# A bidirectional RWKV-7 step: the triangular inversion on two partitions a block, and values and keys turned by VectorE and SBUF transfers in place of PE transposes

## The chip, the cores and the metric

The kernel runs on one core of a Trainium2 chip, in float32. The metric is the device time of one execution in microseconds. PE is the matmul engine, DVE the vector engine, ACT the scalar engine, POOL GpSimd, and SP the engine that issues nearly all DMA transfers. Each engine works through its own instructions in the order in which they stand in its program.

## The reference

One layer: h = modulated RMSNorm(x) for 384 tokens (128 of context, 256 latent), z = h @ w_in, then an RWKV-7 scan in both directions over 32 heads of 64, a short convolution, gates and output projections.

```python
def step(S, inp):
    r_t, w_t, k_t, v_t, a_t, b_t = inp
    sa = jnp.einsum('dbhij,dbhj->dbhi', S, a_t)
    S = S * w_t[..., None, :] + sa[..., :, None] * b_t[..., None, :] + v_t[..., :, None] * k_t[..., None, :]
    y = jnp.einsum('dbhij,dbhj->dbhi', S, r_t)
    return S, y
...
y_a = (y.astype(h.dtype) * jax.nn.silu(g_a)) @ w_out_a
y_b = (b_gate * u * jax.nn.silu(g_b)) @ w_out_b
merged = jax.nn.sigmoid(m_a) * y_a + jax.nn.sigmoid(m_b) * y_b
return merged @ w_o, S_fin
```

The scan is computed by chunks of 64 tokens (6 chunks, two directions, two heads: 24 triangular systems of 64 x 64 in a block of two heads). Each needs the inverse of a unit triangular matrix, which is built from 32 x 32 blocks.

## The kernel before

**The stream.** All large projections run through one stream of matmuls on PE (class Stream). It works on pairs of 128 columns: rk (receptance and keys of a block), gv (gate of the block and values of the next), ma, mb, bc, bx, bg, gb and so on, h against 2048 rows of weights. A step is three matmuls on a 128 x 128 tile (mm3: hi*hi, hi*lo, lo*hi; lines 81 to 83), a pair has 32 steps. The weights of half a pair are loaded into a tile raw (two buffers, wload, L101 or, in two pieces, L104), and split quarter by quarter into whi (ACT, L88) and wlo (DVE, L89), three buffers each: wlo_gv_0_0 is the first quarter of gv, wlo_gv_1_0 the third. A step needs both parts of its quarter.

**The blocks.** The scan is done for 16 blocks of two heads, b = 0 to 15. For each the main loop runs generators that put their own matmuls between the steps of the stream; a yield of n lets n steps go. prep_b makes the masked products A (pA on PE, A on DVE), stores their 32 x 32 diagonal blocks to DRAM (ui), loads them as U with one diagonal block on each of 48 partitions, inverts all 48 with 30 pairs of DVE instructions (a product into ut, a sum into U), stores the result (uo) and loads it back into A; x11 takes its transposes. prep_c turns the values (6 transposes on PE to pv, copied by ACT to sav) and the scaled keys (10 transposes to pb, copied to bt). prep_a of the next block follows when gv is done (pl, pn), and the stream is let go until the window of 80 steps between prep_b and the scan is full. Then scan runs: pav, pH, pX and the chains of po, pq and pu.

**What sets the order.** PE's order is written out by hand (manual_schedule). DVE, ACT, POOL and SP are ordered when the program is built: the builder's scheduler takes, at each moment of its own reckoning, the earliest written instruction that it holds ready, and issue_after keeps one behind another. That order is fixed in the program; the chip does not change it. In the loop 160 steps make a block: rk and gv are the first two whole pairs after the second pA, then three of the other pairs.

Results of rk are taken by take_shifted: ACT copies the product to zs and scales it to r or k (L417, L418), DVE adds the neighbours with four instructions each (L422, L424). v comes from gv's second half in the same way.

## Time and profile before

| | us |
|---|---|
| median of 3 runs (2234.74 to 2237.2) | 2236.57 |
| the profiled execution, its own time | 2234.36 |
| its span, first to last instruction | 2232.6 |
| DVE inversion, products (480) and sums (480), busy | 154.8 and 154.5 |
| ACT copies of pv and pb, busy | 30.3 and 25.1 |
| PE transposes to pb, and to pv (values, reversed values), busy | 27.9, 7.8 and 7.9 |
| landing of U (192 KB), uo (192 KB) and A (48 KB), median | 5.1, 4.7 and 3.6 |
| mean granted clock of PE | 0.998 |

Times of an engine's groups are unions of their instructions and overlap with other groups of the same engine. In the rows of a timeline the first number is the start in us from the beginning of the span, the second the length; a bracket at the end gives idle time of the engine before the row and what ended it. SPq rows are the issue of transfers, not their flight. Line numbers are those of the kernel before.

### The profile page before, as it was taken

What the parts mean: (1) busy time and instruction counts of PE and PEld (TensorE: products, weight loads), DVE (VectorE), ACT (ScalarE), POOL (GpSimd) and SP (SyncE); (2) the same over time, 40 slices, a digit from 0 to 9 for tenths busy, and PEclk for the clock granted to TensorE, in tenths of its full rate; (3) what the DMA queues carried; (4) which work ended last, traced back from release to release, by engine and by line L of the source; (5) the groups of instructions that cost most, each with busy time, mean ns of one, the idle gap of its engine ahead of it and who ended that gap; (6) DMA issues with size and microseconds to landing.
All of it is one profiled execution on the core that took longest, in us unless ns stands there. A gap on an engine that the chain in (4) does not pass through costs nothing.

```text
span 2232.6 us, 40518 instructions
## 1 busy us (share of the span) xinstructions
PE 2173.1 (97%) x16020; PEld 2062.7 (92%) x16020; DVE 1553.3 (70%) x3240; ACT 1013.5 (45%) x1784; POOL 115.7 (5%) x113
## 2 busy tenths in 40 slices
PE   5999999999999999999999999999999999999998
PEld 3589999999999999999999999999999999998988
DVE  3259567787878878777878787887777785444354
ACT  4245435454545454444445454546454633333333
POOL 2000000000000000000000000000000000000000
PEclk9999999999999999999999999999999999999999
DMA  9974454444343435343444434344445464886633
GB/s 338 346 211 128 131 141 116 116 117 118 108 132 107 130 100 131 106 130 100 121 108 127 112 107 133 107 122 126 124 118 139 144 196 143 294 281 233 220 132 113
DMA packets 426574, 335.25 MB, mean 150 GB/s; under 512 B 82496, under 2 KB 408720, under 8 KB 425488
## 3 DMA queue, kind: packets, MB, share of 16 engines
q1 hardware_dynamic: 424896, 330.91, 50.2%
q8 instruction: 126, 2.06, 0.4%
q10 hardware_dynamic: 432, 1.57, 0.2%
q14 instruction: 64, 0.52, 0.1%
q0 software_dynamic: 1056, 0.19, 0.1%
HBM read 305.80 MB, written 26.21 MB: 149 GB/s over the span
## 4 chain that ended last, share of the span: by engine, by line
PE 74%; DVE 12%; DMA 6%; ACT 4%; issue 2%; SPq 1%; POOL 0%; POOLq 0%; DVEq 0%; ACTq 0%
DMA raw_adah<-in_ada_w_dram 4%; PE d_rk L81 3%; PE d_rk L82 3%; PE d_rk L83 3%; PE d_gv L81 3%; PE d_gv L82 3%; PE d_gv L83 3%; PE d_oa L81 2%; PE pA L703 2%; PE d_oa L83 2%; PE d_oa L82 2%; PE d_mb L81 2%; PE d_mb L83 2%; PE d_mb L82 2%; PE d_bc L81 2%
## 5 line engine op out<-in xcount | busy, mean ns | idle before, releaser
L724 DVE TENSOR_TENSOR ut<-U 48x30 f32<-48x30 f32 (+14 forms) x480 | 154.8, 323 | 18.3 <-DMA U<-ui 5.5
L81 PE MATMUL d_rk<-h_hi,whi_rk 128*128 128x384 f32 x480 | 161.7, 337 | 0.6 <-ACT lst L554 0.6
L726 DVE TENSOR_TENSOR U<-U,ut 48x30 f32<-48x30 f32 (+14 forms) x480 | 154.5, 322 | 11.1
L81 PE MATMUL d_gv<-h_hi,whi_gv 128*128 128x384 f32 x480 | 160.6, 335 | 0.0
L82 PE MATMUL d_rk<-h_lo,whi_rk 128*128 128x384 f32 x480 | 160.5, 334 | 0.0
L83 PE MATMUL d_rk<-h_hi,wlo_rk 128*128 128x384 f32 x480 | 160.4, 334 | 0.0
L83 PE MATMUL d_gv<-h_hi,wlo_gv 128*128 128x384 f32 x480 | 160.4, 334 | 0.0
L82 PE MATMUL d_gv<-h_lo,whi_gv 128*128 128x384 f32 x480 | 160.4, 334 | 0.0
L88 ACT CAST whi_gv<-raw_gv 128x1024 fp32r<-128x1024 f32 (+1 forms) x64 | 64.0, 999 | 139.6 <-PE d_rk L82 100.0
L88 ACT CAST whi_rk<-raw_rk 128x1024 fp32r<-128x1024 f32 x60 | 63.0, 1054 | 110.8 <-PE d_rk L82 34.7
L89 DVE TENSOR_TENSOR wlo_rk<-raw_rk,whi_rk 128x1024 fp32r<-128x1024 f32 x60 | 72.9, 1218 | 45.3 <-ACT whi_rk L88 35.6
L81 PE MATMUL d_bc<-h_hi,whi_bc 128*128 128x384 f32 x256 | 92.2, 360 | 0.0
L81 PE MATMUL d_gb<-h_hi,whi_gb 128*128 128x384 f32 x256 | 92.2, 360 | 0.0
L81 PE MATMUL d_bg<-h_hi,whi_bg 128*128 128x384 f32 x256 | 92.2, 360 | 0.0
L81 PE MATMUL d_bx<-h_hi,whi_bx 128*128 128x384 f32 x256 | 92.1, 360 | 0.0
L81 PE MATMUL d_ma<-h_hi,whi_ma 128*128 128x384 f32 x256 | 91.6, 358 | 0.0
L81 PEld LDWEIGHTS d_rk<-h_hi,whi_rk 128*128 128x128 f32 x480 | 90.1, 188 | 0.9 <-ACT lst L554 0.9
L81 PE MATMUL d_mb<-h_hi,whi_mb 128*128 128x384 f32 x256 | 90.4, 353 | 0.0
L81 PEld LDWEIGHTS d_gv<-h_hi,whi_gv 128*128 128x128 f32 x480 | 90.1, 188 | 0.2
L81 PE MATMUL d_ob<-ybh,whi_ob 128*128 128x384 f32 x256 | 88.4, 345 | 2.0 <-DVE smb L521 1.0
L82 PEld LDWEIGHTS d_rk<-h_lo,whi_rk 128*128 128x128 f32 x480 | 90.2, 188 | 0.0
L82 PEld LDWEIGHTS d_gv<-h_lo,whi_gv 128*128 128x128 f32 x480 | 90.1, 188 | 0.0
(315 smaller groups left out, 6548.4 us busy)
## 6 DMA issues: line engine op xcount, KB each, us to landing
raw_adah<-in_ada_w_dram SPq DMA_DIRECT2D x64, 512.0 KB, 8.7
raw_rk<-in_w_in_dram SPq DMA_DIRECT2D x60, 512.0 KB, 5.3
raw_gv<-in_w_in_dram SPq DMA_DIRECT2D x60, 512.0 KB, 4.9
raw_ma<-in_w_in_dram SPq DMA_DIRECT2D x16, 1024.0 KB, 5.6
raw_mb<-in_w_in_dram SPq DMA_DIRECT2D x16, 1024.0 KB, 5.6
raw_bc<-in_w_in_dram SPq DMA_DIRECT2D x16, 1024.0 KB, 5.5
raw_bx<-in_w_in_dram SPq DMA_DIRECT2D x16, 1024.0 KB, 5.4
raw_bg<-in_w_in_dram SPq DMA_DIRECT2D x16, 1024.0 KB, 5.5
```

Source lines behind the costliest of these rows:

```text
L81: TE.matmul(out, wh, xh, start=start, stop=False)
L82: TE.matmul(out, wh, xl, start=False, stop=False)
L83: TE.matmul(out, wl, xh, start=False, stop=stop)
L88: S.copy(hi[0:rows], src)
L89: V.tensor_tensor(lo[0:rows], src, hi[0:rows].bitcast(F32), ALU.subtract)
L703: TE.matmul(pas[h, n // 4 * 4][:, n % 4, :], bk[hss[h], n, :], pr[hss[h], n, :], start=True, stop=True)
L724: V.tensor_tensor(tv, U[:, 0:s, s:s + 1].broadcast_to([48, s, w]), U[:, s:s + 1, s + 1:].broadcast_to([48, s, w]), ALU.mult)
L726: V.tensor_tensor(U[:, 0:s, s + 1:], U[:, 0:s, s + 1:], tv, ALU.add)
```

## The change

The inversion uses two partitions for a 32 x 32 block. un holds all rows of the block on partitions 0 to 47 and again on 64 to 111; ux holds the even rows of it on the first and the odd rows on the second set, so each of the 30 column steps works on half the rows in one instruction over 112 partitions. There are two loads of un, two of ux and two stores of uo, where there were one and one. The values and the scaled keys are turned in 32 x 32 blocks by DVE (vt, and bks in place), and 8 transfers for sav and 16 for bt, issued by SP, put the blocks in place within SBUF. The transposes to pv and pb and their ACT copies are gone. prep_c gives 24, 16 and 1 steps to the stream in place of its seven; the window stays 80.

```diff
+        box["raw"] = x.ins
...
+    un = sp.tile([112, 32, 32], F32, tag="un", name="un")
+    ux = sp.tile([112, 16, 32], F32, tag="ux", name="ux")
...
+        vt = sp.tile([P, 2, T], F32, tag="vt", name=f"vt_{b}")
+        with tc.issue_after(last):
+            for d in range(2):
+                V.transpose(vt[:, d], v_[b][:, ::-1] if d else v_[b][:])
+            for d in range(2):
+                V.transpose(flat(bks[:, d]), flat(bks[:, d]))
...
-        nc.sync.dma_start(U[:], ui[:].rearrange("d e i s t -> (d e i) s t"))
+        for g in range(2):
+            nc.sync.dma_start(un[64 * g:64 * g + 48], ui[:].rearrange("d e i s t -> (d e i) s t"))
+        for g in range(2):
+            o["loaded"] = nc.sync.dma_start(ux[64 * g:64 * g + 48], ui[:].rearrange(
+                "d e i (m g) t -> (d e i) m g t", g=2)[:, :, g, :]).ins
+        ut = sp.tile([112, 128], F32, tag="ut", name=f"ut_{b}")
         for s in range(1, 31):
-            w = 31 - s
...
+            w, m = 31 - s, (s + 1) // 2
+            tv = ut[:, 0:m * w].rearrange("p (a b) -> p a b", b=w)
+            V.tensor_tensor(tv, ux[:, 0:m, s:s + 1].broadcast_to([112, m, w]),
+                            un[:, s:s + 1, s + 1:].broadcast_to([112, m, w]), ALU.mult)
+            V.tensor_tensor(ux[:, 0:m, s + 1:], ux[:, 0:m, s + 1:], tv, ALU.add)
+        for g in range(2):
+            dg = ux[64 * g:64 * g + 48].rearrange("p a b -> p (a b)")[:, g:512:34]
+            V.tensor_scalar(dg, dg, 1.0, None, ALU.add)
+            nc.sync.dma_start(uo[:].rearrange("d e i (m g) t -> (d e i) m g t", g=2)[:, :, g, :],
+                              ux[64 * g:64 * g + 48])
+        x11 = un[0:64, 0:24, :]
...
-                TE.transpose(pv[:, q, :], src[:, q * P:(q + 1) * P], ident)
...
-                    TE.transpose(pb[:, n - n0, :], o["bk"][d][:, n, :], ident)
-                S.copy(bt[:, NCH * d + n0:NCH * d + n1, :], pb[:, 0:n1 - n0, :])
...
+        with tc.issue_after(o["loaded"]):
+            for e in range(2):
+                for q in range(4):
+                    nc.sync.dma_start(sav[C + 32 * e:C + 32 * e + 32, :, 32 * q:32 * q + 32],
+                                      x[32 * q:32 * q + 32, :, e, :])
+        x = o["bks"][:].rearrange("p d n t -> p (d n) t")
+        for p in range(4):
+            if p % 2 == 0:
+                yield (24, 16)[p // 2]
+            with tc.issue_after(box["raw"]):
+                for q in range(4):
+                    nc.sync.dma_start(bt[32 * p:32 * p + 32, :, 32 * q:32 * q + 32],
+                                      x[32 * q:32 * q + 32, :, 32 * p:32 * p + 32])
```

PE's order loses the transposes and keeps the rest, with the first block's pl and pn some steps later. The order of the other engines moves in more places, shown here for the eleventh block (b = 10), where bg follows gv.

On DVE, around the end of the pair rk: r_ and k_ are the shifts of rk's results, ut with U (or ux) the inversion, wlo_gv_0_0 and wlo_gv_0_1 the splits of the first two quarters of gv. wlo_gv_0_0 stands nine rows ahead of the first of these. Before:

```order
L89 TENSOR_TENSOR wlo_gv_0_1_13421<-raw_gv_0_13413,whi_gv_0_1_13420 128x1024
L726 TENSOR_TENSOR U_13198<-U_13198,ut_13200 48x14x17
L724 TENSOR_TENSOR ut_13200<-U_13198 48x240
L726 TENSOR_TENSOR U_13198<-U_13198,ut_13200 48x15x16
L422 SCALAR_TENSOR_TENSOR r_13460<-zs_13461,par,r_13460 128x127
L724 TENSOR_TENSOR ut_13200<-U_13198 48x240
L424 SCALAR_TENSOR_TENSOR r_13460<-zs_13461,par,r_13460 128x127
```

And now, from the second shift of k on:

```order
L425 SCALAR_TENSOR_TENSOR k_13455<-zs_13456,par,k_13455 128x127
L746 TENSOR_TENSOR ux<-ux,ut_13200 112x9x13
L423 SCALAR_TENSOR_TENSOR k_13455<-zs_13456,par,k_13455 128x255
L744 TENSOR_TENSOR ut_13200<-ux,un 112x120
L425 SCALAR_TENSOR_TENSOR k_13455<-zs_13456,par,k_13455 128x255
L746 TENSOR_TENSOR ux<-ux,ut_13200 112x10x12
L606 TENSOR_TENSOR lo_bs_13496<-kd_0_12705,bsh_13495 128x384
L744 TENSOR_TENSOR ut_13200<-ux,un 112x110
L89 TENSOR_TENSOR wlo_gv_0_0_13384<-raw_gv_0_13380,whi_gv_0_0_13383 128x1024
L746 TENSOR_TENSOR ux<-ux,ut_13200 112x10x11
L89 TENSOR_TENSOR wlo_gv_0_1_13388<-raw_gv_0_13380,whi_gv_0_1_13387 128x1024
```

Both splits have moved from ahead of the shifts to behind the last of them; 20 rows of the inversion follow, and behind those stand both splits of gv's second half.

On ACT, from the end of rk to the start of bg: zs, r, k and v are the copies and scalings of rk's and gv's results, whi the casts. Before:

```order
L88 CAST whi_gv_0_0_13416<-raw_gv_0_13413 128x1024
L88 CAST whi_gv_0_1_13420<-raw_gv_0_13413 128x1024
L417 COPY zs_13461<-d_rk_0_13342 128x384
L418 ACTIVATE r_13460<-d_rk_0_13342,cm 128x384
L88 CAST whi_gv_1_0_13493<-raw_gv_1_13490 128x1024
L417 COPY zs_13481<-d_rk_1_13343 128x384
L418 ACTIVATE k_13480<-d_rk_1_13343,cm 128x384
L88 CAST whi_gv_1_1_13497<-raw_gv_1_13490 128x1024
L613 ACTIVATE kk_13618<-k_13480,par 128x384
L88 CAST whi_bg_0_0_13551<-raw_bg_0_13549 128x1024
L88 CAST whi_bg_0_1_13555<-raw_bg_0_13549 128x1024
L439 ACTIVATE ga_13595<-d_gv_0_13488 128x384
```

And now, from the copy of k on:

```order
L419 ACTIVATE k_13455<-d_rk_1_13320,cm 128x384
L605 CAST bsh_13495<-kd_0_12705 128x384
L88 CAST whi_gv_0_0_13383<-raw_gv_0_13380 128x1024
L88 CAST whi_gv_0_1_13387<-raw_gv_0_13380 128x1024
L619 ACTIVATE kk_13611<-k_13455,par 128x384
L88 CAST whi_gv_1_0_13468<-raw_gv_1_13465 128x1024
L88 CAST whi_gv_1_1_13472<-raw_gv_1_13465 128x1024
L440 ACTIVATE ga_13588<-d_gv_0_13463 128x384
L418 COPY zs_13604<-d_gv_1_13464 128x384
L419 ACTIVATE v_13603<-d_gv_1_13464,cm 128x384
L621 ACTIVATE sq_13613<-kk_13611 128x384
L605 CAST sqh_13615<-sq_13613 128x384
```

The casts of gv's first half moved from ahead of rk's copies to behind them, and those of bg from ahead of gv's copies to behind them: whi_bg_0_0 is the next row after these. On DVE wlo_bg_0_0 stands behind the four shifts of v and lo_sq in the same way. In the blocks 1, 4, 8, 12, 13 and 14 kk stands ahead of whi_gv_0_0.

On SP, from the loads of gv to those of bg. Before:

```order
L104 DMA raw_gv_0_13413<-in_w_in_dram 128x8x128
L719 DMA U_13198<-ui_13102 48x1024
L104 DMA raw_gv_0_13413<-in_w_in_dram 128x8x128
L104 DMA raw_gv_1_13490<-in_w_in_dram 128x8x128 x2
L101 DMA raw_bg_0_13549<-in_w_in_dram 128x8x256
L101 DMA raw_bg_1_13634<-in_w_in_dram 128x8x256
L101 DMA raw_gb_0_13797<-in_w_in_dram 128x8x256
L729 DMA uo_13103<-U_13198 48x1024
L621 DMA lraw_0_14770<-in_w_dram 96x2x128
L734 DMA A_13104<-uo_13103 32x12x32 x4
```

And now:

```order
L738 DMA ux<-ui_13095 48x16x32 x2
L782 DMA sav_13280<-vt_13191 32x12x32 x8
L104 DMA raw_gv_0_13380<-in_w_in_dram 128x8x128
L791 DMA bt_13281<-bk_13033 32x12x32 x8
L104 DMA raw_gv_1_13465<-in_w_in_dram 128x8x128
L750 DMA uo_13096<-ux 768x1x32 x2
L104 DMA raw_gv_1_13465<-in_w_in_dram 128x8x128
L791 DMA bt_13281<-bk_13033 32x12x32
L756 DMA A_13097<-uo_13096 32x12x32 x4
L791 DMA bt_13281<-bk_13033 32x12x32 x7
L101 DMA raw_bg_0_13542<-in_w_in_dram 128x8x256
L101 DMA raw_bg_1_13627<-in_w_in_dram 128x8x256
```

The store uo stood behind the first load of gb; now it stands ahead of the second piece of gv's second half, and the return of the inverse (A) and seven bt transfers stand ahead of bg's loads.

## The prediction

> **What bounds the kernel now.** I read the page's shares and chain first, then who waits for whom on PE, then one block of the main loop in order of time.

> ```profile
> span 2232.6 us, 40518 instructions
> PE 2173.1 (97%) x16020; PEld 2062.7 (92%) x16020; DVE 1553.3 (70%) x3240; ACT 1013.5 (45%) x1784; POOL 115.7 (5%) x113
> PE 74%; DVE 12%; DMA 6%; ACT 4%; issue 2%; SPq 1%; POOL 0%; POOLq 0%; DVEq 0%; ACTq 0%
> PE pada L292 <- DMA raw_adah<-in_ada_w_dram: 22.4, 16, 9.4
> PE po L804 <- DVE st L833: 7.6, 9, 1.6
> 1255.00:1315.00 60.00, 60.00 (x464) 58.87 (x463) 48.92 (x115) 26.96 (x44) 4.38 (x3) 1.00 0.52 142
> ```

> The first three rows are from the page, the next two from the view of waits (total, times, longest), the last from the windows view (stretch, its length, busy time of PE, PEld, DVE, ACT, POOL, granted clock, DMA share, GB/s). PE is the bound, and in the stretch from 1255 to 1315 us, which holds the window of the eleventh block, it is busy for all 60 of 60 us. Its waits lie in the prologue, and in the loop the largest sum is 7.6 us. So whatever PE no longer does is a gain, whatever DVE, ACT or SP no longer do is none, and anything that PE newly waits for is a loss in full. The question is whether weights still arrive in time.

> ```profile
> 1264.55 0.42 PEld L763 LDWEIGHTS pv<-cs,v 128*128 128x128 f32 x3
> ...
> 1269.01 0.19 PEld L81 LDWEIGHTS d_rk<-h_hi,whi_rk 128*128 128x128 f32 x1
> ...
> 1285.62 0.19 PEld L81 LDWEIGHTS d_gv<-h_hi,whi_gv 128*128 128x128 f32 x1
> ```

> This is PE's weight-load timeline (start, length). The pair rk has 32 steps in 16.61 us, 0.519 us a step, and gv follows. I call R the moment when gv may begin (1285.62 here) and count from it below.

> **What goes: the transposes.** From the first pv load to the first rk load are 4.46 us, in which five steps of the stream (2.60 us) also ran. Sixteen transposes thus hold PE for 1.87 us a block, **29.9 us** in 16 blocks. DVE's inversion rows get about half as long and ACT loses its copies of pv, pb and vr; neither engine is the bound, so I count nothing for them. VectorE's new transposes stand ahead of the inversion while its loads are on their way, so they too cost nothing; without that cover they would cost some 3 us a block (two of 384 and two of 768 columns, against 0.56 us for one of 384).

> ```profile
> L737 DVE STREAM_TRANSPOSE x<-A 32x384 f32<-32x384 f32 x32 | 17.4, 558 | 25.3 <-DMA A<-uo 25.1
> ```

> **What is moved: first wait, at R.** Before, gv's first quarter is cast and split while rk is still running, and the copies and shifts of rk come after.

> ```profile
> 1277.54 1.05 ACT L88 CAST whi_gv<-raw_gv 128x1024 fp32r<-128x1024 f32 x1 [3.10 <-PE d_rk L82]
> ...
> 1283.91 0.48 ACT L417 COPY zs<-d_rk 128x384 f32<-128x384 f32 x1 [1.20 <-PE d_rk L83]
> 1284.28 0.59 ACT L418 ACTIVATE r<-d_rk,cm 128x384 f32<-128x384 f32 x1
> ...
> 1279.08 1.21 DVE L89 TENSOR_TENSOR wlo_gv<-raw_gv,whi_gv 128x1024 fp32r<-128x1024 f32 x1
> ...
> 1285.79 0.33 DVE L422 SCALAR_TENSOR_TENSOR r<-zs,par,r 128x127 f32<-128x127 f32 x1
> ...
> 1288.37 1.21 DVE L89 TENSOR_TENSOR wlo_gv<-raw_gv,whi_gv 128x1024 fp32r<-128x1024 f32 x1
> 1289.50 0.39 DVE L724 TENSOR_TENSOR ut<-U 48x234 f32<-48x234 f32 x1
> ...
> 1292.06 0.37 DVE L724 TENSOR_TENSOR ut<-U 48x220 f32<-48x220 f32 x1
> ```

> In the changed order the cast on ACT and the split on DVE of that quarter stand behind the copies and the eight shifts of r and k, which need the end of rk. PE cannot finish gv's first step without the split, so a wait is certain. Its length: r is ready at 1284.87, R - 0.75. Eight shifts with eight inversion rows took 6.27 us from 1285.79 to 1292.06, less 1.13 for the split among them, 5.14; the inversion rows in between, of 117 to 128 elements, are now some 0.28 us instead of 0.39 long (0.29 at 130 and 0.26 at 108 elements in the groups below), so 4.3. Then lo_bs 0.55, one inversion row 0.28, the split 1.21: the end is R + 5.6. PE does two of the first three matmuls (0.35) meanwhile: **5.25 us**. The thirty inversion rows ahead take about 8.4 us (0.25, between the rows of 30 and 130 elements, and a gap of 0.03 each) from the last split of rk, near R - 9.9; should the loads, now 576 KB instead of 192, make them more than 0.8 us later, the rest lengthens the wait. Bounds 5.0 to 6.9, the upper one for six blocks where ACT's kk, which needs the shifts, stands ahead of the cast too.

> ```profile
> L726 DVE TENSOR_TENSOR U<-U,ut 48x130 f32<-48x130 f32 x32 | 9.2, 287 | 1.1
> L726 DVE TENSOR_TENSOR U<-U,ut 48x108 f32<-48x108 f32 x32 | 8.4, 263 | 1.1
> L726 DVE TENSOR_TENSOR U<-U,ut 48x30 f32<-48x30 f32 x32 | 6.2, 194 | 0.9
> L605 DVE TENSOR_TENSOR lo_bs<-kd,bsh 128x384 fp32r<-128x384 f32 x16 | 8.7, 547 | 0.3 <-ACT bsh L604 0.3
> ```

> **Second wait, in the middle of gv.** SP issues in order. Before, three more weight loads stand ahead of the store uo; now uo, which waits for the whole inversion, stands ahead of the second piece of raw_gv_1 (in some blocks of both).

> ```profile
> 1266.64 10.33 SPq L104 DMA_DIRECT2D raw_gv<-in_w_in_dram  x3
> 1284.70 9.26 SPq L101 DMA_DIRECT2D raw_bg<-in_w_in_dram  x2
> 1301.81 0.37 SPq L101 DMA_DIRECT2D raw_gb<-in_w_in_dram  x1
> 1302.42 0.38 SPq L729 DMA_DIRECT2D uo<-U  x1
> ...
> 1308.02 1.86 SPq L734 DMA_DIRECT2D A<-uo  x4
> ...
> raw_gv<-in_w_in_dram SPq DMA_DIRECT2D x60, 512.0 KB, 4.9
> ...
> raw_bg<-in_w_in_dram SPq DMA_DIRECT2D x16, 1024.0 KB, 5.5
> ...
> ui<-A SPq DMA_DIRECT2D x64, 48.0 KB, 2.1
> ```

> After R + 5.6 come one row (0.24), a split (1.13 from start to start), twenty rows of 110 down to 15 elements (0.255 each with the gap, 5.1) and the diagonal (0.18): the inversion ends at R + 12.3. Two issues of uo (0.38 each), 4.9 until the piece has landed (the median from issue to landing, last column of the DMA view), cast 1.05, split 1.21: R + 20.2. PE, resumed at R + 5.6, needs it 16 steps (8.3) later, at R + 13.9: **6.3 us**. Bounds 5.5 to 8.5: the landing may be a little quicker, or it queues behind uo's two transfers of 96 KB in 128-byte pieces, as ui<-A has them (48 KB, landed in 2.1).

> **Third wait, at the end of gv.** The next pair's first quarter now stands behind gv's copies on ACT and behind the shifts of v on DVE; before, both cast and split were done by 1297.3.

> ```profile
> 1303.41 0.47 ACT L417 COPY zs<-d_gv 128x384 f32<-128x384 f32 x1
> 1303.78 0.59 ACT L418 ACTIVATE v<-d_gv,cm 128x384 f32<-128x384 f32 x1
> 1304.25 0.53 ACT L615 ACTIVATE sq<-kk 128x384 f32<-128x384 f32 x1
> 1304.81 0.51 ACT L604 CAST sqh<-sq 128x384 fp32r<-128x384 f32 x1
> ```

> From product to copy 0.37 (r's product ends four steps ahead of R, 1283.54, its copy starts at 1283.91), copies to sqh 1.91, cast 1.05, split 1.21, less 0.35 of matmuls: **4.2 us**. The raw load behind it is issued after A<-uo (5.6 us after uo before, so near R + 17.9 to 19.8) and seven bt transfers (0.45 each, as for A<-uo): R + 23, and lands 5.5 later, at R + 28.5. gv ends there too, and the cast wants the load 2.3 us after that, so it is covered by some 2 us; beyond that it adds to the wait. Bounds 3.9 to 6.0.

> **The clock after a wait.** Waits of 4 to 7 us do not occur in the loop before. The nearest rows are in the prologue:

> ```profile
> 16.56 1.94 PE L292 MATMUL pada<-raw_adah,condw_pro 128*32 128x512 f32 x8 [9.35 <-DMA raw_adah<-in_ada_w_dram]
> 18.43 3.09 PE L335 MATMUL pe<-cs,xt 128*128 128x128 f32 x16
> 21.45 1.06 PE L292 MATMUL pada<-raw_adah,condw_pro 128*32 128x512 f32 x8
> 22.45 1.97 PE L335 MATMUL pe<-cs,xt 128*128 128x128 f32 x16
> 25.50 1.07 PE L292 MATMUL pada<-raw_adah,condw_pro 128*32 128x512 f32 x8 [1.09 <-DMA raw_adah<-in_ada_w_dram]
> ```

> After 9.35 us without work, the same two groups take 5.03 instead of 3.03 us, 2.0 us lost; after 1.09 us nothing is lost. A loss after the first wait only shortens the second, whose end is set by SP. The second wait (6.3) is nearer to 9.35 than to 1.09, so I take 2.0; the third (4.2) is nearer to 1.09, so nothing. Ends 0 and 4.0 a block. [...]

> **Sum.** 5.25 + 6.3 + 4.2 + 2.0 - 1.87 = 15.9 us a block. The first two blocks and the last have other pairs and another order, but there too splits stand behind the whole inversion and loads behind uo, so I give them the same: 16 x 15.9 = 254. The profiled execution took 2234.4; 2488 on its scale, and with the 2.2 us by which the median of the runs stands above it, **2490 us**. The ends of all terms give 12.5 and 23.5 a block, 2436 to 2612.

> **Rivals.** (1) The waits hide and only the transposes count: 2236.6 - 29.9 = 2207, faster. For it: PE is at 97% and PE's own order loses nothing but the transposes. It would need gv's first split to end by R, and it stands behind rows that start no earlier than R - 0.75; and the late piece of raw_gv_1 to land by R + 11.6, which asks for an inversion that ends by R + 6. 7%. Nothing measurable, gains and waits in balance: 2%. (2) SP's part is covered, because the inversion ends early or the piece lands fast: only the first and third waits, too short for the clock: 5.25 + 4.2 - 1.87 = 7.6 a block, 2358. Against it: twenty rows, an issue and a landing lie between. 8%. (3) The clock falls after every wait: 4.0 instead of 2.0 a block, 2522. For it the prologue's row, against it that its wait was longer. [...] 13%. (4) The 24 new transfers a block, each 48 KB in 128-byte pieces like ui<-A, hold up weight loads beyond the 2 us of cover, 7 us a block: about 2600. For it: the DMA share is 0.52 already; against it ui<-A lands in 2.1 us (its row stands with the loads, above). 8%.

> That the change doesn't do what it says I rule out: the transposes are gone from PE's order.

> **How the numbers follow.** The forecast has 62%. The range of 2385 to 2590 holds it and rival (3), and leaves out (1), (2) and most of (4). A difference under 0.2%, about 4.5 us, can't be told from no change. Faster 0.07, same 0.02, slower 0.91.

> **What would show it.** PE should show, as its largest waits, d_gv L83 on DVE wlo_gv, some 5 us in each block, d_gv on the cast of its third quarter, some 6 us, and the first steps of the next pair, some 4 us; PE's share should fall to near 87%. SP should wait for ux ahead of uo while raw_gv is behind it. If PE shows no waits at R, the step on the order is wrong; if only the second is missing, the one on SP; if waits agree and the time is higher, the clock or the transfers.

## The result and the profile after

The changed kernel takes **2550.83 us** (median of 4 runs, 2550.34 to 2553.44), the kernel before 2236.51; the ratio is 1.1406, with an interval of 1.1392 to 1.1421. It is slower by 314 us. The forecast was 2490, with a range of 2385 to 2590.

The page's span and busy time, then the view of cores (span, mean granted clock):

```profile
span 2549.3 us, 40472 instructions
PE 2259.6 (89%) x15764; PEld 2122.2 (83%) x15764; DVE 1538.3 (60%) x3320; ACT 949.6 (37%) x1640; POOL 116.6 (5%) x115
core 0: 2549.3 us, clock 0.944
```

PE has 256 instructions less and is nevertheless busy for longer: 2259.6 us against 2173.1. It is also idle for longer: 289.7 us (span less busy) against 59.5. So the 316.7 us of the span divide into 230.2 of idle time and 86.5 of busy time, and since the transposes should have taken some 30 us off the busy time, about 116 us come from the slower clock, 0.944 in place of 0.998 (an estimate; experiment 9 below runs the same PE instructions at a clock of 0.996 in 2149.3 us, and by that it is 110). This division is the first thing to read: waits, and what the clock does behind them, are two separate losses.

Who waits for whom, on PE, ACT and SP (total, times, longest):

```profile
PE d_gv L81 <- ACT whi_gv L88: 121.5, 27, 14.8
PE d_gv L83 <- DVE wlo_gv L89: 24.2, 27, 2.2
PE d_bg L81 <- ACT whi_bg L88: 8.9, 3, 3.0
PE d_bg L83 <- DVE wlo_bg L89: 1.9, 3, 0.6
...
ACT whi_gv L88 <- DMA raw_gv<-in_w_in_dram: 198.5, 14, 15.8
...
SPq L750 <- DVE ux L746: 206.1, 16, 14.0
```

The pair gv waits for its casts and splits about twice in a block, and bg, like each pair that follows gv, once. ACT waits for raw_gv because SP stands for up to 14 us at uo, in all 16 blocks.

The eleventh block in order of time, PE first (start, length, in brackets the idle time before and what ended it):

```profile
1479.33 0.34 PE L83 MATMUL d_rk<-h_hi,wlo_rk 128*128 128x384 f32 x1
1482.06 0.44 PE L81 MATMUL d_gv<-h_hi,whi_gv 128*128 128x384 f32 x1 [2.40 <-ACT whi_gv L88]
1482.34 0.34 PE L82 MATMUL d_gv<-h_lo,whi_gv 128*128 128x384 f32 x1
1484.78 0.69 PE L83 MATMUL d_gv<-h_hi,wlo_gv 128*128 128x384 f32 x1 [2.10 <-DVE wlo_gv L89]
...
1499.81 0.44 PE L81 MATMUL d_gv<-h_hi,whi_gv 128*128 128x384 f32 x1 [4.15 <-ACT whi_gv L88]
1501.07 0.69 PE L83 MATMUL d_gv<-h_hi,wlo_gv 128*128 128x384 f32 x1 [0.65 <-DVE wlo_gv L89]
...
1513.71 0.45 PE L81 MATMUL d_bg<-h_hi,whi_bg 128*128 128x384 f32 x1 [2.95 <-ACT whi_bg L88]
1514.97 0.69 PE L83 MATMUL d_bg<-h_hi,wlo_bg 128*128 128x384 f32 x1 [0.64 <-DVE wlo_bg L89]
```

A step of the stream starts a matmul every 0.173 us, so R, the end of rk, is 1479.50. The first wait ends at 1484.78; two matmuls (0.35) were done in it, and 4.93 us are lost. The last matmul of gv's first half starts at 1495.32, so the next was due at 1495.49, and PE goes on fully at 1501.07: 5.23 lost. The last of gv's second half starts at 1510.42, and in the same reckoning the third wait costs 4.03. Three waits, at the three places, 14.2 us together.

Behind each wait the same matmuls come every 0.32 us. The windows view of the three stretches (stretch, length, busy PE, PEld, DVE, ACT, POOL, granted clock, DMA share, GB/s) and of the whole block:

```profile
1484.78:1490.80 6.02, 6.02 (x19) 6.02 (x20) 5.42 (x20) 0.00 (x0) 0.00 (x0) 0.52 0.01 1
1501.07:1504.50 3.43, 3.43 (x12) 3.43 (x12) 2.01 (x3) 0.00 (x0) 0.00 (x0) 0.55 0.51 91
1514.97:1521.30 6.33, 6.33 (x20) 6.33 (x21) 2.64 (x3) 2.06 (x4) 0.00 (x0) 0.51 0.53 166
1482.00:1606.60 124.60, 111.00 (x803) 106.86 (x803) 80.93 (x185) 46.03 (x85) 5.71 (x4) 0.93 0.45 111
```

PE is busy without a gap in the first three, at a granted clock of 0.52, 0.55 and 0.51. They lose 2.7, 1.5 and 2.9 us (19, 11 and 20 matmuls start in them, each due every 0.173 us), 7.1 together. The block from one start of gv to the next takes 124.6 us, where the eleventh block took 105.0 before (gv's first matmuls at 1285.79 and 1390.80): 19.6 more, of which 14.2 + 7.1 - 1.9 explain 19.4.

SP and ACT at the same place:

```profile
1464.40 7.50 SPq L782 DMA_DIRECT2D sav<-vt  x8
1471.95 0.61 SPq L104 DMA_DIRECT2D raw_gv<-in_w_in_dram  x1
1472.66 5.23 SPq L791 DMA_DIRECT2D bt<-bk  x8
1477.98 0.56 SPq L104 DMA_DIRECT2D raw_gv<-in_w_in_dram  x1
1491.45 1.26 SPq L750 DMA_DIRECT2D uo<-ux  x2
1492.76 0.79 SPq L104 DMA_DIRECT2D raw_gv<-in_w_in_dram  x1
...
1498.71 2.00 ACT L88 CAST whi_gv<-raw_gv 128x1024 fp32r<-128x1024 f32 x2 [15.24 <-DMA A<-uo]
```

SP issues nothing from 1478.54 to 1491.45, when the inversion ends (R + 11.95); the last piece of gv goes out only then, and the cast of the third quarter starts at 1498.71. The bracket names A<-uo, a wait put down to the transfer that came last by the profile; the cast reads raw_gv.

### The profile page after: what moved, and what is told of

Read it like the earlier page. It is cut to its first block, busy times and chain, and to the rows that moved or that the text cites. A ratio compares the mean times of both kernels' runs of the same rounds, so it can differ in the third digit from the quotient of the medians.

```text
span 2549.3 us, 40472 instructions
## 1 busy us (share of the span) xinstructions
PE 2259.6 (89%) x15764; PEld 2122.2 (83%) x15764; DVE 1538.3 (60%) x3320; ACT 949.6 (37%) x1640; POOL 116.6 (5%) x115
## 5 line engine op out<-in xcount | busy, mean ns | idle before, releaser
L81 PE MATMUL d_gv<-h_hi,whi_gv 128*128 128x384 f32 x480 | 190.2, 396 | 121.5 <-ACT whi_gv L88 121.5
L81 PEld LDWEIGHTS d_gv<-h_hi,whi_gv 128*128 128x128 f32 x480 | 110.1, 229 | 130.3 <-ACT whi_gv L88 130.1
L83 PE MATMUL d_gv<-h_hi,wlo_gv 128*128 128x384 f32 x480 | 188.9, 394 | 24.2 <-DVE wlo_gv L89 24.2
L82 PE MATMUL d_gv<-h_lo,whi_gv 128*128 128x384 f32 x480 | 185.0, 385 | 0.0
L81 PE MATMUL d_rk<-h_hi,whi_rk 128*128 128x384 f32 x480 | 160.4, 334 | 0.6 <-ACT lst L555 0.6
L83 PE MATMUL d_rk<-h_hi,wlo_rk 128*128 128x384 f32 x480 | 160.4, 334 | 0.0
L82 PE MATMUL d_rk<-h_lo,whi_rk 128*128 128x384 f32 x480 | 160.3, 334 | 0.0
L89 DVE TENSOR_TENSOR wlo_gv<-raw_gv,whi_gv 128x1024 fp32r<-128x1024 f32 (+1 forms) x64 | 72.8, 1150 | 133.1 <-ACT whi_gv L88 125.2
L88 ACT CAST whi_gv<-raw_gv 128x1024 fp32r<-128x1024 f32 (+1 forms) x64 | 60.7, 991 | 221.8 <-DMA raw_gv<-in_w_in_dram 198.5
L83 PEld LDWEIGHTS d_gv<-h_hi,wlo_gv 128*128 128x128 f32 x480 | 109.2, 227 | 35.9 <-DVE wlo_gv L89 35.9
L744 DVE TENSOR_TENSOR ut<-ux,un 112x30 f32<-112x30 f32 (+7 forms) x480 | 119.5, 249 | 19.0 <-DMA ux<-ui 5.4
L746 DVE TENSOR_TENSOR ux<-ux,ut 112x30 f32<-112x30 f32 (+7 forms) x480 | 119.4, 249 | 14.1
L88 ACT CAST whi_rk<-raw_rk 128x1024 fp32r<-128x1024 f32 x60 | 63.0, 1053 | 144.2 <-PE d_rk L82 36.2
L82 PEld LDWEIGHTS d_gv<-h_lo,whi_gv 128*128 128x128 f32 x480 | 109.7, 229 | 0.0
L81 PE MATMUL d_ob<-ybh,whi_ob 128*128 128x384 f32 x256 | 89.0, 348 | 19.5 <-ACT whi_ob L88 18.5
L81 PE MATMUL d_bg<-h_hi,whi_bg 128*128 128x384 f32 x256 | 93.6, 366 | 8.9 <-ACT whi_bg L88 8.9
L81 PE MATMUL d_ma<-h_hi,whi_ma 128*128 128x384 f32 x256 | 92.6, 362 | 8.9 <-ACT whi_ma L88 8.9
L81 PE MATMUL d_bx<-h_hi,whi_bx 128*128 128x384 f32 x256 | 92.2, 360 | 8.9 <-ACT whi_bx L88 8.9
L89 DVE TENSOR_TENSOR wlo_rk<-raw_rk,whi_rk 128x1024 fp32r<-128x1024 f32 x60 | 72.7, 1214 | 44.8 <-ACT whi_rk L88 43.1
L81 PE MATMUL d_bc<-h_hi,whi_bc 128*128 128x384 f32 x256 | 92.1, 360 | 5.9 <-ACT whi_bc L88 5.9
L81 PE MATMUL d_gb<-h_hi,whi_gb 128*128 128x384 f32 x256 | 92.0, 360 | 5.9 <-ACT whi_gb L88 5.9
L83 PE MATMUL d_ma<-h_hi,wlo_ma 128*128 128x384 f32 x256 | 88.8, 347 | 5.6 <-DVE wlo_ma L89 5.6
## 6 DMA issues: line engine op xcount, KB each, us to landing
raw_adah<-in_ada_w_dram SPq DMA_DIRECT2D x64, 512.0 KB, 8.7
raw_rk<-in_w_in_dram SPq DMA_DIRECT2D x60, 512.0 KB, 5.3
raw_gv<-in_w_in_dram SPq DMA_DIRECT2D x60, 512.0 KB, 4.8
raw_ma<-in_w_in_dram SPq DMA_DIRECT2D x16, 1024.0 KB, 5.7
raw_mb<-in_w_in_dram SPq DMA_DIRECT2D x16, 1024.0 KB, 5.6
raw_bc<-in_w_in_dram SPq DMA_DIRECT2D x16, 1024.0 KB, 5.5
raw_bx<-in_w_in_dram SPq DMA_DIRECT2D x16, 1024.0 KB, 5.6
raw_bg<-in_w_in_dram SPq DMA_DIRECT2D x16, 1024.0 KB, 5.5
```

Source lines behind the costliest of these rows:

```text
L81: TE.matmul(out, wh, xh, start=start, stop=False)
L82: TE.matmul(out, wh, xl, start=False, stop=False)
L83: TE.matmul(out, wl, xh, start=False, stop=stop)
L88: S.copy(hi[0:rows], src)
L89: V.tensor_tensor(lo[0:rows], src, hi[0:rows].bitcast(F32), ALU.subtract)
L744: V.tensor_tensor(tv, ux[:, 0:m, s:s + 1].broadcast_to([112, m, w]), un[:, s:s + 1, s + 1:].broadcast_to([112, m, w]), ALU.mult)
```

## The experiments

All times are medians of 2 to 8 runs; the kernel before, run beside them, gave 2236.8 to 2239.2.

| kernel | us | ratio to before | interval |
|---|---|---|---|
| changed kernel | 2550.8 | 1.1406 | 1.1392 to 1.1421 |
| 1 uo behind gv's loads | 2465.0 | 1.1020 | 1.0988 to 1.1052 |
| 2 sav behind gv's first loads | 2557.1 | 1.1432 | 1.1398 to 1.1465 |
| 3 v behind the next pair's split | 2481.4 | 1.1093 | 1.1061 to 1.1125 |
| 4 all three | 2467.9 | 1.1033 | 1.1001 to 1.1065 |
| 5 transfers issued by ACT | 2288.1 | 1.0225 | 1.0205 to 1.0246 |
| 6 transfers issued by POOL | 2273.0 | 1.0159 | 1.0139 to 1.0180 |
| 7 inversion alone | 2239.0 | 1.0008 | 0.9998 to 1.0019 |
| 8 turning alone | 2465.3 | 1.1019 | 1.0997 to 1.1041 |
| 9 POOL, behind the inversion's loads | 2209.9 | 0.9874 | 0.9859 to 0.9888 |
| 10 as 9, values only | 2225.8 | 0.9943 | 0.9927 to 0.9960 |
| 11 as 9, old inversion | 2212.8 | 0.9884 | 0.9868 to 0.9901 |

### 1. The store of the inverse behind the loads

```diff
-            nc.sync.dma_start(uo[:]...[:, :, g, :], ux[64 * g:64 * g + 48])
...
+            if p == 2:
+                with tc.issue_after(box["raw"]):
+                    for g in range(2):
+                        nc.sync.dma_start(uo[:]...[:, :, g, :], ux[64 * g:64 * g + 48])
+                for e in range(2):
+                    for d in range(2):
+                        nc.sync.dma_start(blocks(A, d, e), uo[d, e].rearrange("i s t -> s i t"))
```

> One edit: the stores uo (and the return A behind them) are written after the loads of gv's second half, so that on SP they stand behind both pieces of raw_gv_1; the orders of DVE and ACT in blocks 2 to 14 stay as in the changed kernel. Theory (SP's order makes the second wait): in the eleventh block's kind the second wait ended 12.7 us of lost time behind the end of rk, of which the first wait (4.9) and its slow clock (2.4) are part; without it 7.3 are left and the slow clock behind the second wait (about 2.0) goes too: 7.4 a block, some 100 us, near 2445. PE's wait at the third quarter of gv is gone. Rival (the load lands late for its own sake, by contention with the 24 small transfers): the wait stays, 2550.

Measured 2465.0, 86 us less. The wait in the middle of gv is gone, as the theory had it. 20 of the 106 us expected came back at the next place: the wait in front of the next pair grew from 2.95 to about 5 us. PE and ACT in the ninth block of this run:

```profile
1221.76 0.69 PE L81 MATMUL d_bc<-h_hi,whi_bc 128*128 128x384 f32 x1 [4.78 <-ACT whi_bc L88]
...
1220.66 1.99 ACT L88 CAST whi_bc<-raw_bc 128x1024 fp32r<-128x1024 f32 x2 [1.73 <-DMA raw_bc<-in_w_in_dram]
```

gv now ends earlier, but the next pair's load still stands behind uo, A and the bt transfers, and ACT waits for it. In the changed kernel that load lands 3 to 6 us before its cast can start (4.7 in the eleventh block: 1507.92 against 1512.62); this cover is used up.

### 2. The first load ahead of the sav transfers

```diff
-        with tc.issue_after(o["loaded"]):
-            for e in range(2): ...
...
+            if p == 0:
+                with tc.issue_after(box["raw"]):
+                    for e in range(2): ...
```

> One edit: the eight sav transfers are written behind the loads of gv's first half. In blocks 2 to 14 the casts and splits of gv's first half then stand ahead of the copies and shifts of rk again, so the first wait should go; uo still stands ahead of raw_gv_1's last piece, and bg's cast behind gv's copies. Theory (the second wait's end is set by the inversion and SP, so the first wait lies inside it): PE reaches the third quarter earlier and waits there for longer, some 12 us in place of 5; little is gained, 2530 to 2550. Rival (the waits add up, each with its slow clock): 4.9 and 2.4 us in 13 blocks, 95 us, near 2455.

Measured 2557.1, nothing gained. The theory holds, though the time lies 7 us above its range: the first wait is gone from blocks 2 to 14, and the second has swallowed it.

```profile
1128.80 0.69 PE L81 MATMUL d_gv<-h_hi,whi_gv 128*128 128x384 f32 x1 [11.91 <-ACT whi_gv L88]
```

That is PE in the eighth block. One wait of 11.9 us stands there in place of 2.40, 1.75, a slow stretch and 4.76. Two waits one behind the other, of which the later has its own cause that PE cannot hasten, do not add up; so the first wait, taken alone, was worth nothing.

### 3. The shifts of v behind the next pair's first split

```diff
+        with ExitStack() as es:
+            if nm == "v":
+                for x in box["first"]:
+                    es.enter_context(tc.issue_after(x))
             shift(t, ps, mi + b, MUP + mi + b, MUN + mi + b)
```

box["first"] holds the first cast and split of the load made last.

> One edit: the copies and shifts of v are held behind the first cast and split of the pair that follows gv, on ACT and on DVE. Only the third wait is touched. Theory (order on ACT and DVE): 4.0 us of wait and about 1.8 of slow clock go in 13 blocks, 75 us, near 2475. Rival (the load of the next pair, which stands on SP behind uo, A and seven bt transfers, lands late anyway): the wait turns into one for that load, 2540 to 2550.

Measured 2481.4, 69 us less, against 75 expected: 5.3 us in each of 13 blocks for a wait of 4.0 and its slow stretch. In the ninth block 0.35 us of waiting are left at bc; the other waits are those in gv.

### 4. The three together

> The three edits together: sav behind gv's first loads, uo behind gv's last load, the copies and shifts of v behind the next pair's first split. The small transfers, the two-partition inversion and the missing PE transposes are all as in the changed kernel. Theory (three waits made by the order are the whole loss): blocks 2 to 14 lose nothing and gain the transposes; the first two blocks and the last keep waits of about 22, 17 and 19 us with their slow clock: 2236 - 30 + 58, near 2265. Rival (the 24 transfers a block hold up weight loads by themselves): waits for raw loads stay in every block, over 2400.

Measured 2467.9, some 200 us more than the theory gave: **this theory fell**. The three waits were taken away, and two others stand in their place in blocks 2 to 14. PE, DVE and ACT in the ninth block:

```profile
1207.07 0.69 PE L83 MATMUL d_gv<-h_hi,wlo_gv 128*128 128x384 f32 x1 [5.25 <-DVE wlo_gv L91]
...
1205.61 0.18 DVE L756 TENSOR_TENSOR ux<-ux,ut 112x15 f32<-112x15 f32 x1
1205.79 2.36 DVE L91 TENSOR_TENSOR wlo_gv<-raw_gv,whi_gv 128x1024 fp32r<-128x1024 f32 x2
...
1221.29 1.99 ACT L90 CAST whi_bc<-raw_bc 128x1024 fp32r<-128x1024 f32 x2 [5.32 <-DMA raw_bc<-in_w_in_dram]
```

The split of gv's third quarter stands on DVE behind the last row of the inversion, and goes the moment that row is done; the next pair's load lands late as in the first experiment. Neither had shown while PE was late for other reasons. So it is not three misplaced rows alone that cost the time: as long as 24 issues on SP stand between the loads, the built order puts other rows ahead of those that PE needs, and on SP real loads do stand behind the inversion. (That the builder does so because it takes the loads for late is argued from its rule, not shown by a run.) What the three edits cured, the next row showed.

### 5 and 6. The same transfers on another queue

```diff
-                    nc.sync.dma_start(sav[...], ...)
+                    nc.scalar.dma_start(sav[...], ...)
...
-                    nc.sync.dma_start(bt[...], ...)
+                    nc.scalar.dma_start(bt[...], ...)
```

For POOL it is nc.gpsimd, and without the two issue_after, whose instructions are SP's.

> The changed kernel with one edit: the 24 transfers of a block to sav and bt are issued by ACT instead of SP; they move the same bytes at about the same time. The built order of SP, DVE and ACT then has gv's casts and splits ahead of rk's copies and shifts, the next pair's ahead of v's, and uo behind all loads of gv and of the next pair, as before the change. Theory (the loss is what 24 issues on SP do to the order, not the transfers): no waits at gv and the next pair, the clock stays up, and PE gains its transposes: 2237 - 30 = 2207, to 2215 with what 24 issues of some 0.5 us delay on ACT. Rival (the transfers themselves, 1.1 MB a block in pieces of 128 bytes, hold up the weight loads): waits for raw loads remain, over 2300.

> The same with the 24 transfers issued by POOL, which is busy for 5% of the span. The order of SP, DVE and ACT is again that of before. Theory (order alone): 2207, as with ACT, and ACT is spared the issues. Rival (POOL's way of issuing costs more per transfer than SP's, and bt comes too late for the scan's pu): 2230 to 2300, with PE waiting at pu or pav for bt or sav.

Measured 2288.1 and 2273.0: of 314 us 263 and 278 are gone with the change of queue. In 6 gv's splits stand among the shifts as they did before the change; in 5 those of its first half do, but those of its second half stand behind the shifts of k. Neither time is 2207, so the transfers, or where they start, cost something too. With ACT as the issuer, in the block that begins near 1080 us:

```profile
1088.61 7.07 ACTq L782 DMA_DIRECT2D sav<-vt  x4
1096.11 1.99 ACT L88 CAST whi_rk<-raw_rk 128x1024 fp32r<-128x1024 f32 x2
...
1097.35 0.18 DVE L749 TENSOR_SCALAR ux<-ux 48x16 f32<-48x16 f32 x1 [7.15 <-DMA ux<-ui]
...
1099.19 1.22 DVE L89 TENSOR_TENSOR wlo_rk<-raw_rk,whi_rk 128x1024 fp32r<-128x1024 f32 x1
```

Four issues hold ACT for 7 us, with rk's casts behind them; and DVE stands 7 us at its first row of the inversion for ux, with rk's split behind that. On POOL the issues hold up nobody (0.62 us each), but the landing of other loads suffers, in the DMA view (KB each, median us to landing):

```profile
raw_gv<-in_w_in_dram SPq DMA_DIRECT2D x60, 512.0 KB, 10.4
...
bt<-bk POOLq DMA_DIRECT2D x256, 48.0 KB, 7.3
...
ux<-ui SPq DMA_DIRECT2D x32, 96.0 KB, 8.3
```

In the changed kernel these three took 4.8, 2.5 and 5.5 us. (bt on POOL's queue takes 4.8 in experiment 9, so its 7.3 is not the queue's alone.) Started at once, the 24 transfers meet un, ux and raw_gv on their way; the inversion begins late, and DVE's rows behind it.

### 7 and 8. Each part of the change alone

In 7, prep_c is that of the kernel before and the VectorE transposes are left out; in 8, the inversion is that of the kernel before.

> Only the first part of the change: the inversion on two partitions a block, with its two loads each of un and ux and two stores uo; values and keys are turned by PE as before. The built order has the splits of gv ahead of the shifts and uo behind the loads. Theory (neither engine is the bound, and the order is unharmed): 2237, within 5. Rival (the larger loads and the four transfers for one cost something of their own): some 5 us in each block, 2300.

> Only the second part: values and keys turned by VectorE and put in place by 24 transfers on SP, with the old inversion on 48 partitions. In the built order uo stands behind the loads of gv, but the loads of the next pair stand behind uo, A and bt, and its first cast and split behind the copies and shifts of v; in blocks 4, 8, 12, 13 and 14 gv's first split stands behind two of the shifts. Theory (the turned issues on SP make the loss, the inversion only adds the second wait): a wait of 4 to 5.4 and 2 of slow clock less 1.9 for the transposes in 13 blocks and some 20 us in the first, 2310 to 2350. Rival (only both parts together are harmful): 2207.

The inversion alone makes no difference (1.0008, 0.9998 to 1.0019), though DVE is busy for 62 us less (1491.2 against 1553.3). The turning alone costs 228 of the 314 us, more than either theory gave. Its trace has waits in the same two places as experiment 4 (d_gv for wlo_gv, 74.8 us in all; the pairs after gv some 60). The split of the third quarter stands behind nearly all of the inversion's rows, which the expectation had left out: it followed only gv's first split. The next pair's cast stands behind the copies of v, as in the changed kernel, and in 11 of the blocks 2 to 14 it waits for its load, issued behind uo and A, for another 0.3 to 3.2 us.

### 9. The transfers on POOL, behind the inversion's loads

```diff
+        o["go"] = G.tensor_copy(scr[64:65], ux[64:65, 0, 0:1]).ins
...
-        with tc.issue_after(o["loaded"]):
+        with tc.issue_after(o["go"]):
...
-                    nc.sync.dma_start(sav[...], ...)
+                    nc.gpsimd.dma_start(sav[...], ...)
...
-            with tc.issue_after(box["raw"]):
+            with tc.issue_after(o["go"]):
...
-                    nc.sync.dma_start(bt[...], ...)
+                    nc.gpsimd.dma_start(bt[...], ...)
```

POOL copies one element of ux, which it can do only when the last load has landed; its 24 issues stand behind that.

> As the run with POOL's queue, with one edit: POOL first copies one element of ux, so that its 24 transfers start only when the last load of the inversion has landed. In the run without it ux took 8.3 us to land and raw_gv 10.4 (5.5 and 4.8 in the changed kernel), the inversion began late, and PE waited for splits, for ga and for the inverse (pH). Theory (what was left of the loss comes from the transfers' meeting the inversion's loads): ux lands in 5 to 6 us, those waits go, 2207 to 2225. Rival (1.1 MB in 128-byte pieces slow whatever load they meet): raw_gv keeps landing in 8 to 10 us, the time stays at 2250 to 2280.

Measured **2209.9**, 0.9874 of the kernel before (0.9859 to 0.9888): faster than both kernels, and within 3 us of what the transposes alone were held to be worth. Its page, its DMA view and its waits on PE:

```profile
span 2207.9 us, 40724 instructions
PE 2149.3 (97%) x15764; PEld 2042.9 (93%) x15764; DVE 1529.0 (69%) x3320; ACT 953.1 (43%) x1640; POOL 357.0 (16%) x515
...
raw_gv<-in_w_in_dram SPq DMA_DIRECT2D x60, 512.0 KB, 4.9
...
bt<-bk POOLq DMA_DIRECT2D x256, 48.0 KB, 4.8
...
ux<-ui SPq DMA_DIRECT2D x32, 96.0 KB, 5.5
...
PE pada L293 <- DMA raw_adah<-in_ada_w_dram: 21.6, 15, 9.3
PE pe L262 <- DVE crow L260: 7.3, 1, 7.3
PE po L824 <- DVE st L853: 6.8, 9, 1.6
```

raw_gv and ux land as in the changed kernel, and PE's largest waits are those of the kernel before. The same bytes, by the same 24 transfers on the same queue, cost 63 us more when they start at once, as in 6. Nothing else differs: in 6 and 9 PE, DVE, ACT and SP work through the same rows in the same order (all 3320 of DVE, 1640 of ACT and 1066 issues of SP), so these 63 us are the moment alone. The transfers still slow what they meet, uo landing in 5.4 us where it took 2.9 in the changed kernel, but there it is covered.

### 10 and 11. Values only, and the old inversion

In 10, the keys are turned by PE (the ten transposes to pb and their copies) and POOL issues only the eight sav transfers. In 11, everything is as in 9, with the inversion of the kernel before and POOL's copy reading U.

> The two-partition inversion, values turned by VectorE and put in place by 8 transfers on POOL behind the last load of the inversion, keys turned by PE as before (10 transposes and their copies, where before there were 16 with the values). Theory (transposes are worth what they hold PE for, and 8 transfers are hidden): 6 of 16 parts of 29.9 us, 11 us, 2226. Rival (the transfers cost as much as the transposes): 2237 or more, with raw_gv landing later than 5 us.

> As the run with POOL's queue behind the inversion's last load, but with the old inversion on 48 partitions (one load U, one store uo), POOL copying one element of U first. Theory (the inversion's form is worth nothing as long as it is hidden): 2210, within 5. Rival (its result is wanted at pH, and the old one ends some 4 us later in a window that has lost 1.9 us of transposes): PE waits at pH for x11, 2215 to 2260.

2225.8 is 12.1 less than the 2237.9 beside it, for 6 of 16 transposes; 9 gains 28.0 for all 16. With the old inversion 2212.8 are left, 3 us more than in 9, which ran beside another set of runs of the kernel before; the ratios, 0.9884 and 0.9874, lie within each other's intervals. The gain comes from the transposes, and the form of the inversion has no share in it that these runs can tell.

## Why the prediction was right, and where it was off

- **Sign and cause.** PE lost time to casts, splits and loads that the built order and SP's queue made late, at the three places named, and SP's wait for ux ahead of uo was there in 16 of 16 blocks. PE's share fell to 89%, near the 87% forecast. Experiments 5, 6 and 9, which leave the transfers' bytes as they are and change who issues them and when, show that the queue and the order are the cause. They do not part the two: when the issues left SP, the order of DVE and ACT changed with it. That the 24 transfers hold up loads by themselves (fourth rival) is wrong for their sum of bytes, as 9 shows, and right where they meet those loads, as 6 shows; but the second cannot be read from the changed kernel, whose raw_gv lands in 4.8 us.
- **Transposes, -1.87 us a block.** In 9 the time from one gv to the next is 103.2 us in the eleventh block (gv's first matmuls at 1266.19 and 1369.41), where it was 105.0: -1.8.
- **VectorE's transposes and the shorter inversion, nothing.** Shown by 7, 9 and 11: no new wait of PE above 2.5 us in all came with them.
- **First wait, 5.25.** 4.93 in the eleventh block. But experiment 2 shows that it was not a term of the sum in its own right: the second wait's end does not depend on it.
- **Second wait, 6.3, its end at R + 20.2.** The inversion ended at R + 11.95, forecast 12.3. But the two issues of uo took 1.26 in place of 0.76, and from the issue of the piece to the cast went 5.95 in place of 4.9, so the wait ended at R + 21.57, 1.4 later. The slow stretch behind the first wait (2.7) lies inside, as the prediction had said; that made the wait itself shorter, 5.23.
- **Third wait, 4.2.** 4.03. Its load landed at R + 28.4, forecast R + 28.5, but gv ended later than forecast, so the cover was 4.7 us and not some 2. In 1, where gv ends earlier, it was gone.
- **The clock, 2.0 a block.** This is the step that failed: "the third (4.2) is nearer to 1.09, so nothing". A wait of 4.0 us lost as much as longer ones: 2.9 us behind the third wait, 1.5 behind the second, 2.7 behind the first, 7.1 in place of 2.0. The nearest row was the wrong one to go by: in the waits measured here the loss does not grow with their length. In experiment 2 the stretch behind 11.9 us (nine matmuls at 0.32, 1.3 us lost) is not longer than those behind 4: by the trace's record the granted clock fell at 1119.69, while PE stood, and was back at 1133.34, 4.5 us after the wait. The row was also no pause of a running PE. Before its 9.35 us PE had done a single matmul of 0.31 us, and the clock record of the kernel before begins only at 20.78 us, near the end of the second slow group, with 1.00: the row priced a start (the author's reading; no run shows the cause). The third rival, the clock falling after every wait, came nearest (behind the three waits of the eleventh block it was 0.52, 0.55 and 0.51), and its price of 2522 was still too low, since it charged 2.0 for two waits.

- **Blocks 0, 1 and 15, taken like the others.** From the third to the fifteenth start of gv a block took 124.7 us where it took 105.0 before, 19.8 more; times 13 that is 257, and 60 of the span's 316.7 are left for those three, 20 each on average (some 42 up to the third start, 18 behind the last). In size that choice was fair; what these three blocks wait for was not taken apart.

So of 62 us between the forecast's 254 and the span's 316.7, idle time gives -22 (230 against 252 for 16 blocks of 15.75) and busy time +84, nearly all of it the clock (110 to 116 against 32).

## What to carry to other kernels

An issue on a queue is not free even if its engine has nothing else to do: what stands behind it in that queue inherits its waits (here SP stood at uo for up to 14.0 us, with the last piece of raw_gv behind it), and a scheduler that orders the other engines by when it believes loads to land can shift rows of theirs too. Where a change adds transfers, look for a queue on which nothing urgent stands, and for the moment at which they meet no load that is waited for; here that turned 14% lost into 1.3% gained with the same work. And do not cure waits one by one: ask of each wait what the next one behind it in time hangs on, for it may end at the same moment without the first.

## What the runs showed of the hardware

PE's slow stretch did not need a long wait here. In experiment 6 a pause of 2.15 us, behind work without a gap, was followed by matmuls at a granted clock of 0.50; in experiment 5 a pause of 2.46 us was followed by none, the clock staying at 1.00. The two pauses lie differently on the steps of 3.413 us on which the clock changes in each trace's record (in the changed kernel's all 82 changes, above). Experiment 6, the pause and the windows view of its step and the next (stretch, length, busy PE, PEld, DVE, ACT, POOL, granted clock, DMA share, GB/s):

```profile
1002.25 0.44 PE L81 MATMUL d_bx<-h_hi,whi_bx 128*128 128x384 f32 x1 [2.15 <-DVE ga L441]
...
999.56:1002.98 3.42, 1.26 (x8) 0.94 (x7) 3.29 (x8) 3.01 (x7) 0.00 (x0) 1.00 0.14 22
1002.98:1006.39 3.41, 3.41 (x13) 3.41 (x12) 2.47 (x7) 0.80 (x1) 0.00 (x0) 0.50 0.99 301
```

And experiment 5:

```profile
1100.46 0.44 PE L83 MATMUL d_rk<-h_hi,wlo_rk 128*128 128x384 f32 x1 [2.46 <-DVE wlo_rk L89]
...
1095.84:1099.25 3.41, 2.16 (x13) 1.84 (x11) 1.37 (x6) 2.25 (x3) 0.00 (x0) 1.00 0.81 188
1099.25:1102.66 3.41, 2.20 (x12) 2.20 (x13) 3.41 (x6) 1.05 (x1) 0.00 (x0) 1.00 0.36 86
1102.66:1106.08 3.42, 3.42 (x22) 3.42 (x21) 3.08 (x13) 1.05 (x1) 0.00 (x0) 1.00 0.94 224
```

The shorter pause lies within one step, which is idle for 2.15 us; the longer one is cut by the steps into 1.25 and 1.21. Counted over the traces of the changed kernel and of experiments 1 to 6, 8, 9 and 11 (from 300 us to 100 us before the end), each of the 199 steps at a granted clock of 1.00 in which PE was idle for 2.0 us or more was followed by a step at 0.50, none of the 5077 with less than 1.0 us was, and of the 123 between these 13 were (in the changed kernel alone all of 40, none of 492 and 1 of 23). A step at 0.50 in which PE was still idle was followed by another: all of 176 with 0.6 us or more, 1 of 184 with less than 0.24 (in the changed kernel all of 28 and none of 35; of the 10 between, 4). The eleventh block loses 1.5 us behind its second wait, where 0.32 us of the first step at 0.50 were idle and no second one followed, and 2.7 and 2.9 behind the others (1.10 and 0.57 idle, two steps each). A step at 0.50 that PE fills costs 1.6 us, an estimate from 0.32 and 0.173 us a matmul. These are counts over the traces; no run moved a pause on the grid to try it.
